# Half-token residual tiles, two pairs of chunks on the first token half ahead of the second half, and operand differences on VectorE

## The chip, the cores and the metric

The kernel runs on one core of a Trainium2 chip. The metric is the device time of one execution in microseconds (us). Three runs of the kernel before gave 1216.2, 1216.57 and 1218.2 us; the median is 1216.57 us. Views of the profile count time from the start of the profiled execution.

## What is computed

One inference step of a one-layer decoder: 1024 prompt tokens and 8 x 4 sample tokens, 1056 columns in all, 1024 features. A mixer (a state-space scan beside sliding-window attention) comes first, then an output projection with a residual add, then a feed-forward block:

```
def hybrid_layer(x, lp, ...):
    ...
    x = x + jnp.concatenate([y_ssd, y_att], axis=-1) @ lp['w_out']
    hn = rmsnorm(x, lp['norm2'])
    u, ffn_conv_new = causal_dwconv(hn @ lp['w_up'], ffn_conv_prev, lp['ffn_conv_w'], lp['ffn_conv_b'])
    gate, val = jnp.split(u, 2, axis=-1)
    x = x + (jax.nn.silu(gate) * val) @ lp['w_down']
```

The change touches the stretch from the output projection to the first chunks of `hn @ w_up`.

## The kernel before

**Layout.** Everything is feature-major: a tile holds 128 features on partitions and tokens along the free axis. The residual stream is eight tiles `acc[m]` of 128 x 1056. The tokens form two halves (`tp` 0 and 1, HT = 528 columns) of two quarters (QC = 264 columns). Each fp32 product is made of three matmuls on TensorE (PE): high by high, high by low, low by high. An operand is split by a copy on ScalarE (ACT), which makes the high part, and a subtraction on VectorE (DVE), which makes the low one.

**Output projection** (`out_piece`, matmuls at L147). A piece is one `m` and one quarter: 24 matmuls of 264 columns into one PSUM bank, then an add into `acc[m]` on VectorE (L771). Most pieces of the first token half stand in a table of steps (`PLAN`), among the last steps of the mixer; after the table follow the rest of the first half, `half_prep(0)`, and the sixteen pieces of the second half. `half_done` writes the finished half tile to DRAM (L833) and adds its square to a running sum (ACT at L839, VectorE at L840).

**Normalization and operands** (`half_prep(tp)`). `half_rstd` sums the squares over features with small matmuls (L845), takes the reciprocal root in short VectorE steps (L134 to L140, L847), and spreads it over partitions with six transposes on TensorE (L852) and two ACT copies (L854). Then eight VectorE instructions scale the half tiles in place (L864). The matrix product `hn @ w_up` is done as a two by two block scheme with seven block products, so seven operands are formed from the four blocks of (feature half) x (quarter): four blocks and differences of them. Each operand has four feature tiles: four ACT copies (L875), four VectorE subtractions (L876); four differences (`minus`, L880, on GpSimd, named POOL in the views) precede each of four operands. All work on 128 x 264 tiles.

**Up projection.** For each of 22 pairs `cp` of output chunks, `up_load` reads two 512 KB weight tiles into two buffers tagged "raw", and `up_operand(cp, j)` makes seven weight operands `au` (four differences and sums on GpSimd at L910 and L912, seven ACT copies at L922, seven VectorE subtractions at L923) in eight rotating slots. `product(cp, tp, j)` is 12 matmuls of 264 columns (L976), j = 0 to 6 for each half; j = 6 is put off until after j = 1 of the next half. Results are read out of PSUM by ACT (L990, L993, L996, L1004) and VectorE (L984, L986, L998) into two tiles `u` of the pair. When both halves are done, `conv` runs over each `u`: one ACT pass (L1016), two VectorE passes of 128 x 1072 (L1018), then SiLU or the final product (L1027).

**What sets the order.** The kernel is traced in program order; a scheduler then places each instruction in the queue of its engine, each queue runs strictly in order, and tiles come out of pools with a fixed number of buffers. The pool `yp` has eight buffers with tag "y"; the tiles `acc`, the tiles `u` and the conv results `c` share them. The program order around the change is: products of pair 0 on half 0, then `half_prep(1)`, then pair 0 on half 1, then pair 1 on both halves, and so on:

```
for cp in range(NPAIR):
    for tp in range(2):
        if (cp, tp) == (0, 1):
            half_prep(1)
```

Of the kernel before, what the change touches and what calls it, by code (L numbers as in the profile page):

```python
# [46 lines left out]
def kernel(ctx, tc, xT, wxbc, wkv, wq, wz, wout, wup, wdn, cols, rows, cst, idm,  # L47
# [711 lines left out]
    def out_load(m):  # L759
        if acc[m] is None:  # L760
            acc[m] = yp.tile([128, T], F32, tag="y", name="acc")
            sp.dma_start(out=acc[m], in_=xT[m])
        w[m] = load_unit(wout[m])

    def out_piece(m, q):
        if w.get(m) is None:
            out_load(m)
        a, b = q * QC, q * QC + QC
        ps = bank()[:, :QC]
        dense(ps, wl(w[m]), lambda h, k: yx[k][h][:, a:b], range(8))  # L770
        dve.tensor_tensor(out=acc[m][:, a:b], in0=acc[m][:, a:b], in1=ps, op=ALU.add)  # L771
# [58 lines left out]
    def half_done(m, tp, first):  # L830

        h = acc[m][:, tp * HT:tp * HT + HT]
# [26 lines left out]
    def half_prep(tp):  # L859

        rb = half_rstd(tp)
        for m in (4, 5, 6, 7, 0, 1, 2, 3):
            h = acc[m][:, tp * HT:tp * HT + HT]
            dve.scalar_tensor_tensor(out=h, in0=h, scalar=col(C_N2 + m), in1=rb, op0=ALU.mult, op1=ALU.mult)  # L864

        def quarter(r, c):
            return [acc[(0 if r else 4) + j][:, (2 * tp + c) * QC:(2 * tp + c) * QC + QC] for j in range(4)]
# [3 lines left out]
        def operand(name, src):  # L871
            hl = [x2p[tp].tile([128, 4, QC], F32R, tag=name + p, name=f"x2{p}") for p in "hl"]
            X2[tp][name] = hl
            for j in range(4):
                act.activation(out=hl[0][:, j], in_=src[j], func=AF.Copy)  # L875
                dve.tensor_tensor(out=hl[1][:, j], in0=src[j], in1=hl[0][:, j].bitcast(F32), op=ALU.subtract)  # L876

        def minus(o, p, q):
            for j in range(4):
                pool.tensor_tensor(out=o[j], in0=p[j], in1=q[j], op=ALU.subtract)  # L880
# [12 lines left out]

    nslot = [0]
# [3 lines left out]
    def up_load(cp):  # L898
        raws[cp] = [wr.tile([128, 1024], F32, tag="raw", name="raw") for _ in range(2)]
        for i in range(2):  # L900
            sp.dma_start(out=raws[cp][i], in_=wup[2 * cp + i])

    def up_operand(cp, j):

        ra, rb = raws[cp]
        a12, a11, a22, a21 = ra[:, 0:512], ra[:, 512:1024], rb[:, 0:512], rb[:, 512:1024]
        if j == 1:
            A[cp, "t"] = pt_.tile([128, 512], F32, tag="t1", name="t1")
        t = A.get((cp, "t"))
        minus = lambda o, p, q: pool.tensor_tensor(out=o, in0=p, in1=q, op=ALU.subtract)  # L910
        if j == 1:
            pool.tensor_tensor(out=t, in0=a21, in1=a22, op=ALU.add)  # L912
# [7 lines left out]
        w = wp.tile([128, 1024], F32R, tag=("uh", "ul")[nslot[0] % 2], name="au")  # L920
# [318 lines left out]
```

## Time and profile before

| | |
|---|---|
| median of three runs | 1216.57 us |
| profiled execution: its own time | 1216.3 us |
| its span, first to last instruction | 1214.5 us |
| mean granted TensorE clock | 0.976 |
| busy share PE / DVE / ACT / POOL | 96% / 71% / 42% / 32% |
| product matmuls of the up projection (L976) | 3696 |

The profiled execution took 1216.3 us, 1.8 us more than the span between its first and its last instruction, and 0.3 us less than the median. In rows of a view, `ps<-x2h,au 128x264 x12 | 1.2, 286 | 0.5 <-ACT u L990` reads: twelve instructions that write `ps` from `x2h` and `au`, 1.2 us busy in all, 286 ns each, 0.5 us of idle time on that engine just ahead of them, ended by the ACT instruction at line 990. A timeline row begins with its start and its length in us; idle time stands in brackets. Matmuls overlap, so their starts and not their lengths set the pace.

### The profile page before, as it was taken

The page shows a single profiled execution, that of the slowest core. Times are in us where ns is not written, and L with a number is a line of the kernel's source. Part 1 is how long each engine was busy: PE and PEld are TensorE (multiplying, and loading weights), DVE is VectorE, ACT ScalarE, POOL GpSimd, SP SyncE. Part 2 cuts the span into 40 slices and gives each one's busy share as a digit, 9 for nine tenths or more (in the row PEclk, how much of TensorE's full clock was granted, in tenths as well). Part 3 has the DMA queues.
Part 4 walks back from the last instruction along what each step waited for, and adds up shares of the span by engine and source line. Part 5 has one row for each costly group of instructions (what it writes and reads, how often), then busy time and mean ns, then how long its engine had stood idle before and what let it go on. Part 6 is the DMA issues. An engine that isn't in the chain of part 4 may idle for free.

```text
span 1214.5 us, 22163 instructions
## 1 busy us (share of the span) xinstructions
PE 1161.0 (96%) x8614; PEld 1113.6 (92%) x8614; DVE 865.3 (71%) x1732; ACT 508.7 (42%) x1013; POOL 385.7 (32%) x511
## 2 busy tenths in 40 slices
PE   8999999989989998499999999999999999999998
PEld 7998888869767998399999999999999999999998
DVE  7678857486797588866866666666666877777764
ACT  7344644454544343454545554554545322112110
POOL 0125444343443042733434343444443011101000
PEclk9999999999988999599999999999999999999999
DMA  8111112132645513022222222222222853423403
GB/s 289 62 62 57 36 49 66 26 105 70 184 138 157 177 54 136 1 71 71 76 84 73 87 72 88 71 88 72 88 72 88 289 182 125 139 89 110 146 9 144
DMA packets 50921, 121.48 MB, mean 100 GB/s; under 512 B 9072, under 2 KB 19824, under 8 KB 50800
## 3 DMA queue, kind: packets, MB, share of 16 engines
q1 hardware_dynamic: 50816, 120.07, 29.3%
q8 instruction: 67, 1.10, 0.4%
q14 instruction: 38, 0.31, 0.1%
HBM read 93.81 MB, written 27.26 MB: 100 GB/s over the span
## 4 chain that ended last, share of the span: by engine, by line
PE 85%; DVE 6%; POOL 3%; DMA 2%; issue 2%; ACT 1%; SPq 0%; POOLq 0%; ACTq 0%
PE ps L976 36%; PE ps L147 34%; PE ps L199 6%; POOL acc L880 2%; PE ps L525 1%; PE sc L503 1%; DVE acc L864 1%; PE yy L653 1%; DVE x2l L876 1%; PE ps L517 1%; PE st L660 1%; PE two L147 1%; PE yy L655 0%; DVE au L923 0%; DMA xr<-in_xT 0%
## 5 line engine op out<-in xcount | busy, mean ns | idle before, releaser
L976 PE MATMUL ps<-x2h,au 128*128 128x264 f32 x2464 | 457.1, 286 | 10.9 <-ACT u L990 6.1
L976 PEld LDWEIGHTS ps<-x2h,au 128*128 128x128 f32 x2464 | 385.8, 190 | 12.2 <-ACT u L990 6.4
L976 PE MATMUL ps<-x2l,au 128*128 128x264 f32 x1232 | 351.1, 286 | 5.3 <-DVE x2l L876 5.3
L976 PEld LDWEIGHTS ps<-x2l,au 128*128 128x128 f32 x1232 | 233.6, 190 | 6.5 <-DVE x2l L876 6.5
L1088 DVE TENSOR_TENSOR acc<-acc,ps 128x352 f32<-128x352 f32 x264 | 131.4, 517 | 66.3 <-PE ps L147 65.7
L147 PE MATMUL ps<-xh,uh 128*128 128x264 f32 (+3 forms) x528 | 164.4, 318 | 8.1 <-ACT xh L182 5.5
L147 PE MATMUL ps<-gl,uh 128*128 128x352 f32 x528 | 170.1, 322 | 0.0
L147 PE MATMUL ps<-gh,ul 128*128 128x352 f32 x528 | 169.9, 322 | 0.0
L147 PE MATMUL ps<-gh,uh 128*128 128x352 f32 x528 | 167.8, 322 | 0.1
L147 PE MATMUL ps<-xl,uh 128*128 128x264 f32 (+3 forms) x528 | 166.3, 315 | 0.6 <-POOL xl L180 0.4
L147 PE MATMUL ps<-xh,ul 128*128 128x264 f32 (+3 forms) x528 | 165.1, 313 | 0.0
L116 ACT ACTIVATE uh<-raw 128x1024 fp32r<-128x1024 f32 (+3 forms) x59 | 55.8, 953 | 189.7 <-PE ps L147 171.2
L1018 DVE SCALAR_TENSOR_TENSOR c<-u,colt,c 128x1072 f32<-128x1072 f32 x88 | 120.0, 1364 | 1.1 <-ACT c L1016 0.8
L147 PEld LDWEIGHTS ps<-xh,uh 128*128 128x128 f32 x528 | 101.8, 195 | 12.4 <-ACT xh L182 5.8
L923 DVE TENSOR_TENSOR au<-raw,au 128x512 fp32r<-128x512 f32 x110 | 76.0, 704 | 43.5 <-ACT au L922 43.4
L147 PEld LDWEIGHTS ps<-xl,uh 128*128 128x128 f32 x528 | 102.8, 195 | 2.6 <-POOL xl L180 0.9
L147 PEld LDWEIGHTS ps<-xh,ul 128*128 128x128 f32 x528 | 102.8, 195 | 1.6 <-issue 0.7
L147 PEld LDWEIGHTS ps<-gl,uh 128*128 128x128 f32 x528 | 99.2, 188 | 0.5 <-DVE gl L180 0.2
L147 PEld LDWEIGHTS ps<-gh,ul 128*128 128x128 f32 x528 | 99.3, 188 | 0.0
L147 PEld LDWEIGHTS ps<-gh,uh 128*128 128x128 f32 x528 | 98.8, 188 | 0.3 <-ACT gh L179 0.3
L922 ACT ACTIVATE au<-raw 128x512 fp32r<-128x512 f32 x110 | 68.4, 625 | 23.1 <-PE ps L976 11.3
L923 DVE TENSOR_TENSOR au<-t,au 128x512 fp32r<-128x512 f32 x44 | 43.5, 988 | 35.4 <-PE ps L976 19.0
(291 smaller groups left out, 1973.3 us busy)
## 6 DMA issues: line engine op xcount, KB each, us to landing
raw<-in_wup SPq DMA_DIRECT2D x44, 512.0 KB, 3.5
gr<-gd SPq DMA_DIRECT2D x22, 528.0 KB, 5.1
gd<-c SPq DMA_DIRECT2D x22, 512.0 KB, 2.6
raw<-in_wdn SPq DMA_DIRECT2D x22, 512.0 KB, 4.2
raw<-in_wout SPq DMA_DIRECT2D x12, 512.0 KB, 3.8
acc<-in_xT SPq DMA_DIRECT2D x8, 528.0 KB, 5.9
accd<-acc SPq DMA_DIRECT2D x16, 264.0 KB, 2.0
acc<-accd SPq DMA_DIRECT2D x8, 528.0 KB, 8.0
```

Source lines behind the costliest of these rows:

```text
L116: act.activation(out=hi, in_=raw, func=AF.Copy)
L147: pe.matmul(out=ps, lhsT=w(a, k), rhs=x(b, k), start=first and k == ks[0] and i == 0, stop=last and k == ks[-1] and i == 2)
L199: pe.matmul(out=ps[:m, :n], lhsT=x[k][c][:, a:a + m], rhs=w[k // nk][b][:, o:o + n], start=k == 0 and i == 0, stop=k == 7 and i == 2)
L503: pe.matmul(out=sb[:, v, c].rearrange("p i k -> p (i k)"), lhsT=qT[a][r, c], rhs=kT[b][r, o:o + 256], start=i == 0, stop=i == 2)
L517: pe.transpose(out=pt[:, h], in_=P[:, h], identity=ident)
L525: pe.matmul(out=po[64 * v:64 * v + 64, 0:256].rearrange("p (c q) -> p c q", c=2), lhsT=(vall[:, t - i] if i or not t else vdif[:, t - 1])[ ...
L880: pool.tensor_tensor(out=o[j], in0=p[j], in1=q[j], op=ALU.subtract)
L922: act.activation(out=w[:, 0:512], in_=src, func=AF.Copy)
L923: dve.tensor_tensor(out=w[:, 512:1024], in0=src, in1=w[:, 0:512].bitcast(F32), op=ALU.subtract)
L976: pe.matmul(out=ps, lhsT=wgt[:, 512 * a + 128 * k:512 * a + 128 * k + 128], rhs=xx[b][:, k], start=opens and k == 0 and i == 0, stop=k == ...
L1018: dve.scalar_tensor_tensor(out=c[:, 0:n], in0=u[:, j:j + n], scalar=col(C_FW + 3 * m + j), in1=c[:, 0:n], op0=ALU.mult, op1=ALU.add)
L1088: dve.tensor_tensor(out=o, in0=o, in1=ps[:, :PC], op=ALU.add)
```

## The change

It does three things.

1. **Half-token tiles.** `acc[m]` of 128 x 1056 is replaced by `hacc[m // 2, tp]`, a tile of 128 x 2 x 528 for two feature tiles and one token half. There are again eight of them, of the same size; the four of the first half carry nothing of the second half. Each half tile is loaded by its own DMA (16 of 264 KB in place of 8 of 528 KB). Copies, subtractions and differences of `half_prep` run over two feature tiles at once: 14 + 14 + 8 instructions of 528 elements in place of 28 + 28 + 16 of 264, for each half.
2. **Order of the pairs.** A list `SETS` of weight sets takes the place of the loop over pairs: set 0 is pair 0 on half 0; set 1 is pair 1 on both halves; set 2 is pair 0 again, on half 1, with its weights loaded and split a second time; from set 3 on each pair is done on both halves as before. `half_prep(1)` stays in program order behind pair 0 on half 0; pair 1 on half 0 now follows it.
3. **Engine.** The differences of `half_prep`, and the differences and sums of the weights of sets 0, 1 and 2, go from GpSimd to VectorE.

The core of the diff:

```diff
+    def half(m, tp):
+        if (m // 2, tp) not in hacc:
+            hacc[m // 2, tp] = yp.tile([128, 2, HT], F32, tag="y", name="acc")
+        return hacc[m // 2, tp][:, m % 2]
...
+        if acc[m] != tp:
+            acc[m] = tp
+            sp.dma_start(out=half(m, tp), in_=xT[m][:, tp * HT:tp * HT + HT])
...
-            for j in range(4):
-                act.activation(out=hl[0][:, j], in_=src[j], func=AF.Copy)
-                dve.tensor_tensor(out=hl[1][:, j], in0=src[j], in1=hl[0][:, j].bitcast(F32), op=ALU.subtract)
+            for j in range(2):
+                h, l = (t[:, 2 * j:2 * j + 2] for t in hl)
+                act.activation(out=h, in_=src[j], func=AF.Copy)
+                dve.tensor_tensor(out=l, in0=src[j], in1=h.bitcast(F32), op=ALU.subtract)
         def minus(o, p, q):
-            for j in range(4):
-                pool.tensor_tensor(out=o[j], in0=p[j], in1=q[j], op=ALU.subtract)
+            for j in range(2):
+                dve.tensor_tensor(out=o[j], in0=p[j], in1=q[j], op=ALU.subtract)
...
+    SETS = [(0, [(0, 0)]), (1, [(1, 0), (1, 1)]), (0, [(0, 1)])]
+    SETS += [(cp, [(cp, 0), (cp, 1)]) for cp in range(2, NPAIR)]
...
+        e = dve if n < 3 else pool
+        minus = lambda o, p, q: e.tensor_tensor(out=o, in0=p, in1=q, op=ALU.subtract)
...
+    for n, (cp, groups) in enumerate(SETS):
+        for g in groups:
+            more = g == groups[-1] and n + 1 < len(SETS)
+            if more:
+                up_load(n + 1)
+            done = n >= 2 if cp == 0 else g[1] == 1
+            for j in range(6):
+                product(n, *g, j)
+                if j == 1 and last:
+                    product(*last[0], 6)
+                    if last[1]:
+                        conv(last[0][1], 1)
+                if more:
+                    up_operand(n + 1, j)
+            if more:
+                up_operand(n + 1, 6)
+            if done:
+                conv(cp, 0)
+            last = (n, *g), done
+            if g == (0, 0):
+                half_prep(1)
```

**Where the queues change.** In the rows below a name before the arrow is written and names behind it are read; `au_...` is one weight operand, `x2h_...` and `x2l_...` the high and low part of a token operand, `ps_...` a PSUM bank. On TensorE before, at the end of `half_rstd(1)`: the transposes (L852) are followed at once by the first product on the second half (`x2h_5790`).

```order
L976 MATMUL ps_5681<-x2l_5114,au_5642 128x264
L976 MATMUL ps_5681<-x2h_5113,au_5642 128x264
L852 MATMUL ps_5772<-idt_85,v2_5757 128x88 x3
L852 MATMUL ps_5777<-idt_85,v2_5757 128x88 x3
L976 MATMUL ps_5880<-x2h_5790,au_5626 128x264
```

Only four of pair 0's seven products on half 0 stand ahead of these transposes in the kernel before. In the changed kernel the transposes (L858) stand in the middle of pair 1's product with `au_5729` on half 0:

```order
L988 MATMUL ps_5862<-x2h_5089,au_5729 128x264
L858 MATMUL ps_5774<-idt_85,v2_5759 128x88 x3
L858 MATMUL ps_5779<-idt_85,v2_5759 128x88 x3
L988 MATMUL ps_5862<-x2h_5089,au_5729 128x264
L988 MATMUL ps_5862<-x2l_5090,au_5729 128x264
L988 MATMUL ps_5862<-x2h_5089,au_5729 128x264
```

All seven products of pair 0 and four and three quarters of pair 1's (141 matmuls) now stand between the output projection and the transposes. Fifteen matmuls further down the first reads of the second half follow (`x2h_5792` is its operand B11, `x2h_5814` its operand B21), with pair 1's last product on half 0 (`au_5749`) behind them:

```order
L988 MATMUL ps_5848<-x2l_5098,au_5746 128x264
L988 MATMUL ps_5848<-x2h_5097,au_5746 128x264
L988 MATMUL ps_5948<-x2h_5792,au_5657 128x264
L988 MATMUL ps_6016<-x2h_5814,au_5712 128x264
L988 MATMUL ps_6083<-x2h_5792,au_5962 128x264
L988 MATMUL ps_5848<-x2h_5105,au_5749 128x264
```

So three single matmuls that need the second half were put ahead of twelve that need only the first. On VectorE before, in `half_prep(1)`: scaling (L864), then subtractions for the low parts, with the differences elsewhere (on GpSimd).

```order
L140 SCALAR_TENSOR_TENSOR v_5757<-rs 88x6
L864 SCALAR_TENSOR_TENSOR acc<-acc,colt,ssum_5204 128x528 x8
L876 TENSOR_TENSOR x2l<-acc,x2h 128x264 x15
L923 TENSOR_TENSOR au<-t_5925,au 128x512
L876 TENSOR_TENSOR x2l<-acc,x2h 128x264 x8
```

And now, with the scaling at L870, the low parts at L883 and the differences at L887:

```order
L140 SCALAR_TENSOR_TENSOR v_5759<-rs 88x6
L935 TENSOR_TENSOR au<-raw,au 128x512
L1010 TENSOR_TENSOR u<-u,ps 128x264
L924 TENSOR_TENSOR t_5993<-raw 128x512
L996 TENSOR_TENSOR u<-s_5902,ps 128x264
L870 SCALAR_TENSOR_TENSOR acc<-acc,colt,ssum_5166 128x528 x8
L996 TENSOR_TENSOR u<-s_5875,ps 128x264
L883 TENSOR_TENSOR x2l<-acc,x2h 128x528 x5
L887 TENSOR_TENSOR acc<-acc 128x2x264
```

Work for weight set 2 (L935, L924) and evictions (L1010, L996) moved in ahead of the scaling, and the differences stand between the low parts.

More of the change, by code (lines that the diff above doesn't have):

```diff
@@ L757, in ssd_split @@
             split(fm[4 * g + j][:, a:b], yx[4 + 2 * g + j], None, a, b)
[L759 to L763, printed above, removed]
+    hacc = {}
+    def half(m, tp):
+        if (m // 2, tp) not in hacc:
+            hacc[m // 2, tp] = yp.tile([128, 2, HT], F32, tag="y", name="acc")
+        return hacc[m // 2, tp][:, m % 2]
     def out_piece(m, q):
+        tp = q // 2
         if w.get(m) is None:
-            out_load(m)
-        a, b = q * QC, q * QC + QC
+            w[m] = load_unit(wout[m])
+        if acc[m] != tp:
+            acc[m] = tp
+            sp.dma_start(out=half(m, tp), in_=xT[m][:, tp * HT:tp * HT + HT])
         ps = bank()[:, :QC]
-        dense(ps, wl(w[m]), lambda h, k: yx[k][h][:, a:b], range(8))
-        dve.tensor_tensor(out=acc[m][:, a:b], in0=acc[m][:, a:b], in1=ps, op=ALU.add)
+        dense(ps, wl(w[m]), lambda h, k: yx[k][h][:, q * QC:q * QC + QC], range(8))
+        o = half(m, tp)[:, (q % 2) * QC:(q % 2) * QC + QC]
+        dve.tensor_tensor(out=o, in0=o, in1=ps, op=ALU.add)
     pcc.__exit__(None, None, None)
@@ L830, in half_done @@
     def half_done(m, tp, first):
-        h = acc[m][:, tp * HT:tp * HT + HT]
+        h = half(m, tp)
         sp.dma_start(out=accd[m][:, tp * HT:tp * HT + HT], in_=h)
@@ L862, in half_prep @@
         for m in (4, 5, 6, 7, 0, 1, 2, 3):
-            h = acc[m][:, tp * HT:tp * HT + HT]
+            h = half(m, tp)
             dve.scalar_tensor_tensor(out=h, in0=h, scalar=col(C_N2 + m), in1=rb, op0=ALU.mult, op1=ALU.mult)
         def quarter(r, c):
-            return [acc[(0 if r else 4) + j][:, (2 * tp + c) * QC:(2 * tp + c) * QC + QC] for j in range(4)]
+            return [hacc[(0 if r else 2) + j, tp][:, :, c * QC:c * QC + QC] for j in range(2)]
         b11, b12, b21, b22 = quarter(0, 0), quarter(0, 1), quarter(1, 0), quarter(1, 1)
@@ L896, with up_load, up_operand @@
     raws = {}
[L898 to L899 removed]
+    def up_load(n):
+        raws[n] = [wr.tile([128, 1024], F32, tag="raw", name="raw") for _ in range(2)]
         for i in range(2):
[L901 to L905 removed]
+            sp.dma_start(out=raws[n][i], in_=wup[2 * SETS[n][0] + i])
+    def up_operand(n, j):
+        ra, rb = raws[n]
         a12, a11, a22, a21 = ra[:, 0:512], ra[:, 512:1024], rb[:, 0:512], rb[:, 512:1024]
         if j == 1:
[L908 to L910 removed]
+            A[n, "t"] = pt_.tile([128, 512], F32, tag="t1", name="t1")
+        t = A.get((n, "t"))
+        e = dve if n < 3 else pool
+        minus = lambda o, p, q: e.tensor_tensor(out=o, in0=p, in1=q, op=ALU.subtract)
         if j == 1:
[L912 removed]
+            e.tensor_tensor(out=t, in0=a21, in1=a22, op=ALU.add)
         elif j == 2:
@@ L960, in u_tiles, with product @@
             U[cp].append(u)
-    def product(cp, tp, j):
-        if j == 0 and tp == 0:
+    def product(n, cp, tp, j):
+        if j == 0 and cp not in U:
             u_tiles(cp)
```

32 lines of the change are left out of this document (7 added, 25 removed).

## The prediction

> **What bounds the kernel now.** I read the page first. Its slices show TensorE (PE) at 90% or more nearly everywhere in the later two thirds, but for one dip, in which the granted clock falls too:
>
> ```profile
> PE   8999999989989998499999999999999999999998
> PEclk9999999999988999599999999999999999999999
> ```
>
> A slice is 30.4 us, so the 4 and the 5 stand at 486 to 516 us. Next I cut that stretch into windows, for the product matmuls alone (L976):
>
> ```profile
> 474.60:479.20 4.60, 4.52 (x36) 4.33 (x36) 1.00 0.57 185
> 479.20:515.13 35.93, 14.36 (x58) 12.05 (x59) 0.62 0.09 33
> 580.00:915.00 335.00, 335.00 (x2748) 335.00 (x2747) 1.00 0.23 80
> ```
>
> The last row gives the undisturbed price: 335.0 / 2748 = 0.1219 us per matmul, with PE busy throughout; nothing before the down projection can be gained there. The first two rows hold 36 + 58 = 94 matmuls in 40.5 us. At the undisturbed price they take 11.5 us. The timeline of PE shows two small things that stay whatever the change does, and what else ended its waits:
>
> ```profile
> 474.62 0.28 PE L976 MATMUL ps<-x2h,au 128*128 128x264 f32 x1
> 481.71 1.10 PE L845 MATMUL ps<-ones,ssum 128*88 128x1 f32 x12 [2.57 <-DVE ssum L840]
> 486.26 0.67 PE L852 MATMUL ps<-idt,v 88*128 88x88 f32 x6 [1.89 <-DVE v L140]
> 488.72 0.59 PE L976 MATMUL ps<-x2h,au 128*128 128x264 f32 x1 [1.79 <-ACT x2h L875]
> 493.36 0.59 PE L976 MATMUL ps<-x2l,au 128*128 128x264 f32 x1 [4.06 <-DVE x2l L876]
> 510.36 0.59 PE L976 MATMUL ps<-x2h,au 128*128 128x264 f32 x1 [6.09 <-ACT u L990]
> ```
>
> Sums and transposes take 1.10 + 0.67 = 1.8 us. So the gap loses 40.5 - 11.5 - 1.8 = **27.2 us**. Two chains make it. One is the statistics and the second half's operands. The other is a buffer: the read-out of the very first product waits for a difference of `half_prep(1)` to release a "y" tile,
>
> ```profile
> 509.92 0.39 ACT L990 ACTIVATE u<-ps 128x264 f32<-128x264 f32 x1 [0.47 <-POOL acc L880]
> ```
>
> although that product's matmuls began at 474.6, when the output projection was done. In between VectorE (DVE) and GpSimd (POOL) do the operands, and the clock is halved:
>
> ```profile
> 488.70:515.10 26.40, 12.64 (x45) 10.52 (x46) 24.70 (x38) 12.78 (x32) 21.41 (x22) 0.50 0.00 1
> L876 DVE TENSOR_TENSOR x2l<-acc,x2h 128x264 fp32r<-128x264 f32 x28 | 18.2, 709 | 1.7 <-ACT x2h L875 1.7
> L880 POOL TENSOR_TENSOR acc<-acc 128x264 f32<-128x264 f32 x16 | 18.1, 1163 | 8.8 <-DVE x2l L876 8.8
> L864 DVE SCALAR_TENSOR_TENSOR acc<-acc,colt,ssum 128x528 f32<-128x528 f32 x8 | 5.5, 764 | 1.2 <-ACT ssum L854 1.2
> ```
>
> (First row: PE 12.64 us, DVE 24.70, POOL 21.41 busy of 26.40, clock 0.50.)
>
> **The change part by part.** *Half-token tiles* take the buffer chain away. The first half's four tiles are free when `half_prep(0)` has read them, and its last subtractions end at 460.6 here:
>
> ```profile
> 459.15 1.45 DVE L876 TENSOR_TENSOR x2l<-acc,x2h 128x264 fp32r<-128x264 f32 x4
> 460.87 0.70 DVE L840 TENSOR_TENSOR ssum<-ssum,sq 128x528 f32<-128x528 f32 x1
> 461.49 1.21 DVE L119 TENSOR_TENSOR ul<-raw,uh 128x1024 fp32r<-128x1024 f32 x1
> ```
>
> Four tiles serve `u` of pairs 0 and 1, so both can be read out during `half_prep(1)`. These rows also price VectorE without GpSimd beside it: 0.36 us per 264 elements, and 0.62 us per 528 (from 460.87 to 461.49). `half_prep` then costs 14 + 8 instructions of 0.62, 13.6 us, on VectorE alone, against 18.2 us of VectorE with 18.1 us of POOL interleaved.
>
> *First half's preparation and the output projection* (430.0 to 474.6): PE never idles there, and VectorE is busy 40.55 of 44.6 us.
>
> ```profile
> 430.00:474.60 44.60, 44.60 (x370) 44.60 (x369) 40.55 (x63) 21.83 (x46) 21.75 (x20) 1.00 0.24 85
> ```
>
> VectorE takes over sixteen differences as eight and set 0's four sums, 12 x 0.62 = 7.4 us, and loses the slow-down of its own subtractions, about 28 x 0.35 = 9.8 us if they slow there as above. I price this at nothing. The cover is PSUM: eight banks (pools of 3 and 5), a piece of 24 x 0.1219 = 2.9 us each. Bounds: -1.5 to +2 us, the latter if VectorE ran behind by 2 us at the end.
>
> *DMA.* Eight more residual loads of half the size, and pair 0's two weight tiles again. Loads of the second half now stand ahead of two output-weight loads on SyncE's queue; those were issued at 404.32 and are first read at 437.49, so I price them at nothing, bounds -0.5 to +1. Slight shifts of pieces within the mixer's last steps: nothing, -1.5 to +1.5.
>
> ```profile
> 404.32 2.26 SPq L115 DMA_DIRECT2D raw<-in_wout  x2
> 437.49 1.06 ACT L116 ACTIVATE uh<-raw 128x1024 fp32r<-128x1024 f32 x1 [0.33 <-PE ps L147]
> ```
>
> *Cover in the new order.* From 474.6 PE has 84 matmuls of pair 0 and 57 of pair 1 ahead of the transposes, and the sums: 474.6 + 141 x 0.1219 + 1.8 = 493.6. Does anything delay it? VectorE's queue between the last eviction of the projection and the scaling holds 14 instructions of 512 elements (0.61 by the rate above) for weight sets 0 to 2, a sum of squares (0.62), five evictions of about 0.4 and thirteen small steps that follow each other by 0.2 (rows below): 8.5 + 0.6 + 2.0 + 2.6 = 13.7 us. The last eviction came at 477.4, VectorE lagging; with less lag it is 475.0, so the queue ends at 488.7 to 491.1 unless it waits.
>
> ```profile
> 476.72 0.76 DVE L771 TENSOR_TENSOR acc<-acc,ps 128x264 f32<-128x264 f32 x2
> 484.67 0.16 DVE L139 TENSOR_TENSOR rs<-rs 88x6 f32<-88x6 f32 x1
> 484.87 0.16 DVE L140 SCALAR_TENSOR_TENSOR rs<-rs 88x6 f32<-88x6 f32 x1
> 511.26 0.42 DVE L998 TENSOR_TENSOR u<-u,ps 128x264 f32<-128x264 f32 x1
> ```
>
> The add at L924 for set 1 is now on VectorE and waits for a weight load; evictions and the statistics are queued behind it.
>
> ```profile
> 476.24 0.33 SPq L901 DMA_DIRECT2D raw<-in_wup  x1
> 478.10 0.33 SPq L901 DMA_DIRECT2D raw<-in_wup  x1
> raw<-in_wup SPq DMA_DIRECT2D x2, 512.0 KB, 4.2
> ```
>
> Even issued as late as here that load lands at 478.1 + 4.2 = 482.3, and the 11 us of the queue behind it end at 493.3, still by the transposes. Term zero, up to +3.
>
> *What is late next.* After the transposes PE has 15 matmuls, to 495.4. Two ACT copies (0.67) end at 494.3; the eight scalings run to 494.3 + 5.5 = 499.8. The first matmul of the second half wants two scalings and an ACT copy of 0.65: 496.3. The second wants B21, whose tiles are scaled fifth and sixth: 494.3 + 6 x 0.69 + 0.65 = 499.1. PE waits from 495.4 to 499.1, less one matmul: **3.6 us** (2 to 6), while twelve matmuls that need neither stand behind.
>
> ```profile
> 486.74 0.67 ACT L854 ACTIVATE ssum<-ps 128x264 f32<-128x264 f32 x2 [5.61 <-PE ps L852]
> 464.44 0.65 ACT L839 ACTIVATE sq<-acc 128x528 f32<-128x528 f32 x1 [1.67 <-DVE acc L771]
> ```
>
> *Operands against products.* From 499.8 VectorE needs 13.6 us for the second half's operands, about 4.3 for seven instructions of set 2 and 1.5 for evictions, 19.4 us; PE has 12 + 168 matmuls, 21.9 us. They are nearly level, so PE waits where an operand comes late. T1 is the clear one: its low part is VectorE's tenth instruction after the scaling, about 506.5, and PE, through B11 and B21, is there at 505. Then each difference, copy and subtraction passes DVE, ACT, DVE. **3.5 us** (0 to 8).
>
> *Convolutions.* Pair 1 and pair 0 now end together, so four convs meet in one stretch where there were two per pair. Eight passes of 1.35 and two products of 1.2 are 13.2 us, with set 3's and 4's subtractions queued among them, inside about 20 us of PE work; PE's queue wants set 3's first low part while three conv passes stand ahead of it. **4 us** (0 to 8).
>
> ```profile
> L1018 DVE SCALAR_TENSOR_TENSOR c<-u,colt,c 128x1072 f32<-128x1072 f32 x71 | 95.8, 1349 | 0.5 <-ACT c L1016 0.3
> L923 DVE TENSOR_TENSOR au<-raw,au 128x512 fp32r<-128x512 f32 x89 | 60.8, 697 | 37.6 <-ACT au L922 37.5
> ```
>
> *Clock.* Two gaps show when it falls. The first has 1.2 us of PE work in 3.2 us, and the next 3.4 us run at half clock:
>
> ```profile
> 422.50:425.70 3.20, 1.21 (x16) 1.00 (x14) 1.14 (x2) 0.64 (x1) 0.00 (x0) 1.00 0.23 84
> 426.30:429.70 3.40, 3.40 (x18) 3.40 (x17) 1.58 (x10) 0.00 (x0) 0.00 (x0) 0.50 0.00 0
> 482.70:488.70 6.00, 2.33 (x20) 1.95 (x19) 4.27 (x15) 1.09 (x3) 1.28 (x1) 0.92 0.00 0
> ```
>
> The second, 2.5 us idle up to 481.7, did not halve it at once (0.92 after). An episode of 3.4 us costs half, 1.7 us. My 3.6 us wait is like the first: **2 us** for one episode and a bit (0 to 6). [...]
>
> **The sum.** New losses: 3.6 + 3.5 + 4 + 2 = 13.1 us. Gain: 27.2 - 13.1 = 14.1 us. From the profiled execution's own 1216.3 us (span 1214.5) that is 1202.2; the median is 0.3 above it, so **1202.5 us**.
>
> **The rivals.** *Covered almost wholly* (gain 18 to 25 us): waits of VectorE and PE overlap and convs hide. Losses of 3.6 and 1 leave 1216.6 - 22.6 = 1194 us. For it: 19.4 against 21.9 us above. Against it: the three single matmuls placed early.
>
> *The half clock stays* (gain 0 to 8 us): PE is fed by VectorE in small portions and never gets a full window of work. Before, 26.4 us at 0.50 is such a stretch. If pair 1's and pair 0's second halves (168 matmuls) all run at half price, they cost 168 x 0.1219 = 20.5 us more, while PE then runs behind VectorE and the waits on operands and convs disappear: 27.2 - 3.6 - 20.5 = 3.1 us gain, 1213.5 us. Against it: between 499 and 521 PE would be busy over 80% of the time, where that stretch has 48%.
>
> *Slower: each early set waits for its weights.* Sets 0, 1 and 2 have one half of products (84 x 0.1219 = 10.2 us) to make the next set's seven operands, where a pair has had 20.5. A weight load (4.2) and two rounds of difference, copy and subtraction (about 2 x 1.9) are 8 us before the fourth operand. If buffers released only when a half ends, three sets would each stall about 10 us: 30 + 3.6 - 27.2 = 6.4 us slower, 1223 us. It decides when raw tiles come free more than 2 us after the sixth operand. Against it: eight slots for seven operands, and the raw rows above, issued while products still ran. That the change does not do what it says is excluded by the queues: pair 1's products do stand ahead of the second half's.
>
> **How the numbers follow.** A measurement of this kernel can tell about 0.2%, 2.4 us, from no change. Forecast (gain 9 to 18): 0.60. Covered: 0.20. Half clock: 0.13, of which 0.05 lie within 2.4 us of no change. Slower: 0.07. So faster 0.60 + 0.20 + 0.08 = 0.88, same 0.05, slower 0.07. The covered case reaches to 1193 but for 0.05 of it; 1213 takes in the forecast's larger losses (27.2 - 23.6 of gain left) and half of the half-clock case. Outside are 0.05, 0.07 and 0.07. Range **1193 to 1213**.
>
> **What would show it.** Right: the read-out of the first product within 1 us of its last matmul; PE without a gap over 2 us until about 495; one wait of 3 to 4 us that ends at an ACT copy of B21; then waits under 2 us on x2l until about 521, and waits on `au` behind conv passes until about 545; half clock for under 5 us. Wrong: PE waiting on `au` of set 1 before 495, a half clock over 10 us, or a PE gap ahead of 474.

## The result, and the profile after

The changed kernel takes 1209.93 us (median of 5 executions, 1206.2 to 1212.86) against 1218.2 us before in the same comparison. The ratio is 0.9933, with a 95% interval from 0.9906 to 0.9959: faster by 0.67%, about 8.3 us. The forecast was 1202.5 us with a range from 1193 to 1213, and a gain of 14.1 us. The profiled execution of the changed kernel takes 1211.65 us (span 1209.9).

The page's slices (30.2 us each) show the deep dip gone. In its place PE has three slices at 8, from 484 to 575 us, and the clock an 8 in the first of them:

```profile
PE   7999999989989999888999999999999999999998
PEclk9999999999988899899999999999999999999999
```

The windows of the product matmuls alone (line 988 in this kernel; columns: stretch, its length, PE busy and matmuls, weight loads, granted clock, DMA share, GB/s):

```profile
477.77:496.30 18.53, 17.56 (x142) 17.19 (x142) 1.00 0.36 122
496.30:507.40 11.10, 7.40 (x37) 6.68 (x38) 0.69 0.01 1
507.40:520.00 12.60, 12.30 (x98) 11.88 (x98) 1.00 0.00 1
520.00:580.00 60.00, 53.37 (x422) 51.68 (x421) 1.00 0.26 85
580.00:915.00 335.00, 335.00 (x2748) 335.00 (x2747) 1.00 0.24 79
```

The first row is the cover: 142 matmuls in 18.5 us, in which only the sums and transposes are missing from a busy PE. The second is the wait that was forecast, with the clock at 0.69. The fourth is the news: in 60 us PE is idle for 6.6 us, in a stretch where the kernel before had no idle time once its dip was over:

```profile
515.13:523.00 7.87, 7.87 (x67) 7.87 (x66) 1.00 0.00 0
523.00:540.00 17.00, 17.00 (x142) 17.00 (x141) 1.00 0.29 95
540.00:580.00 40.00, 40.00 (x330) 40.00 (x330) 1.00 0.20 67
```

The last row of the changed kernel, from 580 us on, has the same busy time and matmuls as before.

To compare runs without what lies ahead of the change, the rest of this text uses one measure: the start of the first product matmul is zero, and the table says when 168, 336 and 672 product matmuls have been issued, that is, when the next one starts (one, two and four pairs of work; at 0.1219 us each they would take 20.5, 41.0 and 81.9 us). "The 168th" below stands for this point, and so on. The next column is the time from the 6900th to the 7100th matmul of the program, the entry of the down projection. All are from the traces, one execution each. The changed kernel, e4 and e5 have the same work up to the 168th and show it at 27.6 us each; the changed kernel and e5 still agree at the 672nd.

| kernel | 168th | 336th | 672nd | down entry | ratio to before, 95% |
|---|---|---|---|---|---|
| before | 49.6 | 70.1 | 111.1 | 28.9 | 1 |
| changed | 27.6 | 51.4 | 99.7 | 32.5 | 0.9933 (0.9906 to 0.9959) |
| e1: old order of pairs | 33.1 | 53.6 | 94.7 | 28.4 | 0.9871 (0.9848 to 0.9895) |
| e2: differences on GpSimd | 33.5 | 64.2 | 109.2 | 32.3 | 1.0014 (0.9998 to 1.0031) |
| e3: preparation written first | 28.4 | 54.3 | 98.9 | 32.1 | 0.9906 (0.9882 to 0.9930) |
| e4: no passes for pair 0 | 27.6 | 51.2 | 95.1 | 32.7 | 0.9902 (0.9883 to 0.9921) |
| e5: slot counter from 1 | 27.6 | 51.4 | 99.7 | 29.1 | 0.9901 (0.9881 to 0.9922) |
| e6: e1 with preparation first | 32.6 | 53.0 | 94.1 | 28.4 | 0.9872 (0.9853 to 0.9891) |
| e7: half tiles alone | 40.9 | 62.3 | 103.3 | 28.4 | 0.9922 (0.9901 to 0.9944) |
| e8: VectorE differences alone | 45.7 | 66.2 | 107.2 | 28.7 | 0.9939 (0.9918 to 0.9960) |
| e10: pair 0's second half later | 27.1 | 49.4 | 95.6 | 28.4 | 0.9892 (0.9870 to 0.9913) |
| e11: e1, weight sums on GpSimd | 34.7 | 55.7 | 96.7 | 29.4 | 0.9887 (0.9864 to 0.9911) |
| e12: e1 with filler matmuls | 31.2 | 53.3 | 94.4 | 28.5 | 0.9875 (0.9858 to 0.9891) |

In the changed kernel the dip gives back 111.1 - 99.7 = 11.4 us, and the entry of the down projection takes 32.5 - 28.9 = 3.6 us of that: 7.8 us, which agrees with the 8.3 us of the medians. The two profiled executions differ by less, 1216.3 - 1211.65 = 4.7 us; where the rest went is told under the term on half tiles below. The table also holds the surprise of this study: e1, which leaves the pairs in their old order, is faster than the changed kernel, and the two intervals don't touch.

### The profile page after: what moved, and what is told of

It is laid out like the page before. It is cut to its first block, busy times and chain, and to the rows that moved or that the text cites. A ratio compares the mean times of both kernels' runs of the same rounds, so it can differ in the third digit from the quotient of the medians.

```text
span 1209.9 us, 22111 instructions
## 1 busy us (share of the span) xinstructions
PE 1162.5 (96%) x8614; PEld 1114.6 (92%) x8614; DVE 864.8 (71%) x1739; ACT 506.2 (42%) x992; POOL 346.8 (29%) x471
## 4 chain that ended last, share of the span: by engine, by line
PE 82%; DVE 7%; DMA 5%; ACT 2%; POOL 1%; issue 1%; SPq 0%; POOLq 0%; ACTq 0%; DVEq 0%
PE ps L147 36%; PE ps L988 32%; PE ps L199 6%; PE ps L525 1%; DMA raw<-in_wup 1%; PE sc L503 1%; DMA xr<-in_xT 1%; DVE au L935 1%; PE yy L653 1%; DVE x2l L883 1%; PE ps L517 1%; PE st L660 1%; DMA Cs<-ead 1%; DMA acc<-accd 1%; DVE ul L119 1%
## 5 line engine op out<-in xcount | busy, mean ns | idle before, releaser
L1102 DVE TENSOR_TENSOR acc<-acc,ps 128x352 f32<-128x352 f32 x264 | 131.5, 517 | 69.9 <-PE ps L147 66.6
L116 ACT ACTIVATE uh<-raw 128x1024 fp32r<-128x1024 f32 (+3 forms) x59 | 55.7, 952 | 192.5 <-PE ps L147 178.6
L935 DVE TENSOR_TENSOR au<-raw,au 128x512 fp32r<-128x512 f32 x115 | 78.7, 699 | 39.9 <-ACT au L934 39.7
L934 ACT ACTIVATE au<-raw 128x512 fp32r<-128x512 f32 x115 | 71.2, 625 | 35.0 <-PE ps L147 9.1
L935 DVE TENSOR_TENSOR au<-t,au 128x512 fp32r<-128x512 f32 x46 | 41.6, 904 | 36.2 <-PE ps L988 19.0
```

The lines of the kernel that those rows point to most:

```text
L116: act.activation(out=hi, in_=raw, func=AF.Copy)
L934: act.activation(out=u[:, 0:512], in_=src, func=AF.Copy)
L935: dve.tensor_tensor(out=u[:, 512:1024], in0=src, in1=u[:, 0:512].bitcast(F32), op=ALU.subtract)
L1102: dve.tensor_tensor(out=o, in0=o, in1=ps[:, :PC], op=ALU.add)
```

## The experiments

Only the lines that carry each edit are shown.

### e1: half tiles and VectorE differences, old order of the pairs

```diff
-    SETS = [(0, [(0, 0)]), (1, [(1, 0), (1, 1)]), (0, [(0, 1)])]
-    SETS += [(cp, [(cp, 0), (cp, 1)]) for cp in range(2, NPAIR)]
+    SETS = [(cp, [(cp, 0), (cp, 1)]) for cp in range(NPAIR)]
```

> Half-token tiles and differences on VectorE as in the changed kernel, but the pairs in the old order (0, 1, 2, ..., each on both halves). The changed kernel's median is 1209.9 us, the one before 1218.2. Measure inside a run, free of what lies ahead: the time from the last matmul of the output projection to the 4000th matmul of the program; 111 us before, 100 in the changed kernel. Theory A (two chains made the gap: the buffer chain is removed by the half tiles, the statistics and operands of the second half are only covered by the order): the read-out of the first product comes within 1 us of its matmuls, PE works through pair 0's first half and then idles and creeps behind VectorE from about 10 us after the projection until about 38 us after it; about 18 us of the 27 stay lost, but no set runs on half the products and the convolutions do not meet, so nothing is given back later: 103 us, time about 1210 (1207 to 1214). Theory B (the order of the pairs carries the gain, the tiles only make it possible): 110 us, 1217. Theory C (the buffer chain was the whole gap): 92 us, 1200.

Measured: 94.7 us to the 672nd product and 1203.8 us (median of 6). That lies between A (which by this measure stood for 103) and C, nearer to C's number, and far from B. C's reason, that the buffer chain was the whole gap, does not hold: e7 below takes that chain away and still needs 103.3 us. In the timeline of PE the chain of the second half is open to view, as A said; two waits make most of it:

```profile
491.72 0.39 PE L987 MATMUL ps<-x2h,au 128*128 128x264 f32 x1 [2.75 <-ACT x2h L882]
495.74 0.59 PE L987 MATMUL ps<-x2l,au 128*128 128x264 f32 x1 [3.63 <-DVE x2l L883]
```

But A took PE to creep behind VectorE until the operands were all done. It doesn't: from the 100th product (23.4 us) to the 168th (33.1) it needs 9.7 us where 8.3 would be full rate. The whole loss is 33.1 - 20.5 - 1.8 (sums and transposes) = 10.8 us, all inside pair 0. Behind it the windows of the product matmuls show full rate, which the changed kernel reaches only at about 578 us:

```profile
523.00:580.00 57.00, 57.00 (x469) 57.00 (x468) 1.00 0.25 85
```

The new order pays less for the chain (27.6 us to the 168th), but 99.7 - 27.6 = 72.1 us for the next 504 products, where e1 needs 61.6. So this order of the pairs, one of the change's three parts, costs 5.0 us on balance.

### e7 and e8: each of the other two parts alone

e7 is e1 with all differences on GpSimd again; e8 is the kernel before with the differences on VectorE.

```diff
-                dve.tensor_tensor(out=o[j], in0=p[j], in1=q[j], op=ALU.subtract)
+                pool.tensor_tensor(out=o[j], in0=p[j], in1=q[j], op=ALU.subtract)
...
-        e = dve if n < 3 else pool
+        e = pool
```

> The half-token tiles alone: old order of the pairs, all differences on GpSimd. From the first product to the 672nd: 111.1 us before, 94.7 with tiles and VectorE differences. Theory A (the two parts each carry some of it: the buffer chain held the first product's read-out for about 35 us, and GpSimd's differences stretch the operands by about 8 us): 102 us (100 to 105), time about 1211. Theory B (with VectorE free of weight sums the old order can stand GpSimd's differences; they only hurt in the new order, where sets 1 and 2 must be ready in half the time): 95 to 97 us, 1205.

> The kernel before with the differences of half_prep and of weight sets 0 to 2 on VectorE: full-token tiles, old order. From the first product to the 672nd: 111.1 us before. Theory A (the read-out of the first product still waits for a difference of half_prep(1) to release its tile, but that difference comes earlier: 16 differences of 0.36 in place of 1.16 us each, subtractions at 0.36 in place of 0.71): the release comes 8 us earlier, 102 to 104 us, time about 1211. Theory B (the buffer chain is what counts, and VectorE becomes the longer chain): 109 to 111 us, 1217 to 1219.

Measured: e7 103.3 us and 1211.0, as A said. e8 107.2 us and 1212.5, between its A and B; the mechanism is A's. In e8 the read-out of the first product still waits for a tile, as the timeline of ScalarE shows; its matmuls began at 477.9:

```profile
508.58 0.68 ACT L991 ACTIVATE u<-ps 128x264 f32<-128x264 f32 x2 [0.52 <-DVE x2l L876]
```

That is 30.7 us after the first matmul, and 35.3 before (509.92 - 474.6): the faster differences bring the release 4.6 us forward, not 8. Alone the tiles give 7.8 us and the engine 3.9; together (e1) 16.4, more than the sum of the two. With the engine alone the wait for the tile stands, as the row shows; with the tiles alone PE still waits for the second half's operands, 2.75 + 3.63 + 2.14 + 2.11 us in its four longest waits.

### e2: differences on GpSimd in the new order

Its edit is that of e7, made in the changed kernel.

> The changed kernel with all operand differences back on GpSimd (those of half_prep and of weight sets 0 to 2). Theory A (GpSimd beside VectorE slows VectorE's subtractions from 0.62 to about 1.2 us per 528 elements, and its own differences take about 2 us each): the second half's operands take about 26 us in place of 17, PE waits on them 6 to 9 us more; from the projection's end to the 4000th matmul 107 us (100 in the changed kernel), time 1216 (1213 to 1221). Theory B (VectorE is the bound between 500 and 523 us, busy 20 of 20, and a GpSimd that stands idle can only relieve it): 97 us, 1206. Also open: the first half's differences at 430 to 475 us, which I priced at nothing; if PE waits there, the stretch from its first product matmul on grows by 1 to 4 us.

Measured: 109.2 us and 1219.7, no gain left at all. A named the mechanism; by the trace it was short by 2 us, and the time lies in its range. B is out. The groups of VectorE and GpSimd between 476 and 530 us show the price (busy us, mean ns of one):

```profile
L883 DVE TENSOR_TENSOR x2l<-acc,x2h 128x528 fp32r<-128x528 f32 x14 | 18.6, 1380 | 0.0
L887 POOL TENSOR_TENSOR acc<-acc 128x528 f32<-128x528 f32 x8 | 13.5, 1703 | 7.9 <-DVE x2l L883 7.9
```

The same rows in the changed kernel, where both run on VectorE:

```profile
L883 DVE TENSOR_TENSOR x2l<-acc,x2h 128x528 fp32r<-128x528 f32 x14 | 9.5, 701 | 0.0
L887 DVE TENSOR_TENSOR acc<-acc 128x528 f32<-128x528 f32 x8 | 5.5, 700 | 0.0
```

Fourteen subtractions take 18.6 us beside GpSimd and 9.5 without, 9.1 us more; the eight differences took VectorE 5.5 us. Eight weight sums went to GpSimd in the same stretch, another 5.5 us, and other VectorE instructions became longer as well. Taken over all groups that both kernels have, by count and mean, VectorE's instructions are longer by 15.7 us, against 11.1 us of work that it was rid of: moving work to an idle engine slowed the busy one by more than it took off. The trace shows both engines' records side by side:

```profile
509.26 1.79 POOL L887 TENSOR_TENSOR acc<-acc 128x528 f32<-128x528 f32 x1
509.79 1.83 DVE L883 TENSOR_TENSOR x2l<-acc,x2h 128x528 fp32r<-128x528 f32 x1
511.01 1.79 POOL L887 TENSOR_TENSOR acc<-acc 128x528 f32<-128x528 f32 x1
```

The difference ends at 511.05, the subtraction 0.57 us later at 511.62, the next difference 1.18 us after that. So the records overlap and their ends alternate, in steps close to what one takes by itself: in the changed kernel such a subtraction takes 0.70 us, and a GpSimd sum 1.29 (the one at 550.43, with VectorE idle from 550.52 on). That reads as if the two took turns here and each record contained a wait for the other; what makes them wait no run shows.

### e11: only the weight sums on GpSimd

```diff
-        e = dve if n < 3 else pool
+        e = dve if n < 1 else pool
```

> Half tiles, old order of the pairs, half_prep's differences on VectorE, the sums of weight sets 1 and 2 back on GpSimd. From the first product to the 672nd: 94.7 us with all of them on VectorE, 103.3 with all on GpSimd. Theory A (any GpSimd sum beside VectorE's operands slows VectorE's subtractions from 0.62 to over 1 us and comes late itself): 96 to 99 us, time about 1206. Theory B (VectorE is saturated from 489 to 512 us, so four sums fewer free 2.4 us there and four sums of GpSimd disturb little): 92 to 93.5 us, time about 1202.

Measured, in e1's order: 96.7 us and 1204.2, A. Three of set 1's four sums on GpSimd fall among the operands' subtractions and take their mean from 704 ns in e1 to 781:

```profile
L883 DVE TENSOR_TENSOR x2l<-acc,x2h 128x528 fp32r<-128x528 f32 x14 | 10.5, 781 | 0.0
```

The 2.0 us by which it is behind e1 can be read from the traces; the medians (1204.2 and 1203.8) can't tell them apart.

### e3 and e6: the second half's preparation written first

e3 is the changed kernel, e6 is e1, each with the same move:

```diff
+    half_prep(1)
     last = None
     for n, (cp, groups) in enumerate(SETS):
...
-            if g == (0, 0):
-                half_prep(1)
```

> The changed kernel with the second half's preparation written ahead of the first set's products, not behind them: its sums and transposes stand about 84 product matmuls behind the projection, not 141, and the scaling ahead of set 2's first steps. Theory A (the 3.5 us wait on scaling and ACT copies, the half clock after it and the 4 us of operands against products all come from the preparation starting too late): scaling starts about 7 us earlier, the wait and the half clock go, the operands run ahead of PE; from the projection's end to the 4000th matmul 91 to 94 us (100 in the changed kernel), time about 1202. Theory B (VectorE is saturated, so what the preparation gains the weight sets 1 and 2 lose): PE waits on au instead, 98 to 101 us, 1208 to 1211. Whatever the result, the stretch up to the projection holds the same instructions in the same order as the changed kernel: if the 4.7 us lost there against the kernel before come from the order, every such run shows them; if from where the half clock happens to fall, they vary by several us from run to run.

> Half tiles and VectorE differences in the old order of the pairs, with the second half's preparation written ahead of pair 0's products, so that the sums stand 43 matmuls behind the projection in place of 60. In the old order the whole loss (94.7 us from the first product to the 672nd, of which 81.9 are matmuls and 1.8 sums) lies within pair 0, and its length is set by the chain sums, root, scaling, operands on VectorE. Theory A: the chain starts 2 us earlier and ends 2 us earlier, 92 to 93 us, time 1202. Theory B (as with the preparation first in the new order, the evictions and set 1's first sum, which waits for its weight load, hold VectorE's queue, so the chain starts no earlier): 94 to 96 us, 1204 to 1205.

Measured: e3 98.9 us and 1208.5; e6 94.1 us and 1204.4. Both numbers are B's. In e3 the scaling does come earlier, but by 2.7 us and not 7 (493.73 against 497.31, which is 16.8 and 19.5 us after the first product), since set 1's subtractions stand between the steps of the root; the 3.5 us wait goes, and PE waits elsewhere:

```profile
489.38 0.39 PE L988 MATMUL ps<-x2h,au 128*128 128x264 f32 x1 [2.58 <-DVE u L996]
516.89 0.39 PE L988 MATMUL ps<-x2l,au 128*128 128x264 f32 x1 [1.36 <-DVE x2l L883]
```

It is 0.8 us behind the changed kernel at the 168th product and 2.9 us at the 336th, and 0.8 us ahead at the 672nd. That is B's account: what one chain gains another loses.

In e6 the number is B's but the chain did what A said. The scaling starts 10.8 us after the first product and not 13.2 as in e1, and the last of the second half's low parts 32.6 us after it and not 34.9, so the whole chain is 2.3 us earlier. After 100 products PE is still 2.2 us ahead of e1, after 168 only 0.5. In between it is the half clock that differs. It lasts two cells in both runs, from 17.5 to 24.3 us after the first product in e6 and from 16.4 to 23.2 in e1, so in e6 it covers a cell in which PE already has work throughout: 17 matmuls, where e1 issues 30 at the same place of its chain (e6 first, then e1; columns as in the windows under e12):

```profile
500.60:504.00 3.40, 3.40 (x17) 3.40 (x17) 3.40 (x6) 1.80 (x4) 0.00 (x0) 0.50 0.00 0
499.60:503.00 3.40, 3.40 (x30) 3.40 (x30) 3.40 (x6) 1.79 (x4) 0.00 (x0) 1.00 0.00 0
```

The 13 matmuls between them are worth 1.6 us at 0.1219 each, about what e6 lost. Whether it would keep the 2.3 us without this cell was not tried.

### e4 and e10: four convolutions that meet

e4 leaves work out, e10 moves pair 0's second half behind pair 2, with the slot counter of e5.

```diff
-        for j in range(1, 3):
+        for j in range(1, 3 if cp else 1):
```

```diff
-    SETS = [(0, [(0, 0)]), (1, [(1, 0), (1, 1)]), (0, [(0, 1)])]
-    SETS += [(cp, [(cp, 0), (cp, 1)]) for cp in range(2, NPAIR)]
-    nslot = [0]
+    SETS = [(0, [(0, 0)]), (1, [(1, 0), (1, 1)]), (2, [(2, 0), (2, 1)]), (0, [(0, 1)])]
+    SETS += [(cp, [(cp, 0), (cp, 1)]) for cp in range(3, NPAIR)]
+    nslot = [1]
```

> The changed kernel without the two VectorE passes (L1030) of each of pair 0's two convolutions: the values of pair 0 are therefore those of the first tap alone. 4 x 1.33 = 5.3 us of VectorE work leave the stretch from 523 to 547 us. Theory A (four convolutions meeting on VectorE delay the low parts of sets 3 and 4 and through them the raw buffers and the next weight loads, 5.7 us of PE between the 3700th and the 4000th matmul): 4 us of it go, from the projection's end to the 4000th matmul 96 us (100 in the changed kernel), time 1206. Theory B (PE waits there on weight loads issued late for other reasons, and on GpSimd's first sum of set 3, 1.7 us): under 1 us goes, 99 to 100 us, 1209 to 1210.

> The changed kernel with pair 0's second half placed behind pair 2 in place of behind pair 1, and the slot counter started at 1 (which gave back 3.5 us at the down projection). Pair 1's and pair 0's convolutions then no longer meet; pair 2's and pair 0's do, but 20 us later, when the second half's operands are long done on VectorE. From the first product to the 672nd: 99.7 us with the slot counter alone. Theory A (what is lost between the 336th and the 672nd product, 7 us, comes from the second half's operands, set 2's and 3's differences and four convolutions falling into the same 25 us on VectorE): 94 to 97 us, time 1203 to 1206. Theory B (the loss belongs to a set that has one half of products to cover the next set's weight load and operands, and to two pairs of convolutions within 30 us, wherever they stand): it moves and stays, 99 to 101 us, time 1208.

Measured: e4 95.1 us to the 672nd and 1206.7; without 5.3 us of VectorE work PE is 4.5 us earlier, where A said 4. e10 95.6 us and 1204.5, again A. By the 1000th product e10 has lost another 0.95 us, so 3.1 us of its 4.1 are for good; it is then still 1.9 us behind e1 (136.6 against 134.7 us). What remains in both, 3.0 us in e4 between the 336th and the 672nd product, isn't from these passes.

### e5: the parity of the weight slots

```diff
-    nslot = [0]
+    nslot = [1]
```

> The changed kernel with the counter of weight slots started at 1 in place of 0. The new order has 23 weight sets of seven operands, 161, an odd number, so the two slot tags end on the other one than with 22 sets; SyncE's queue at the entry of the down projection then issues its weight loads, the convolution's reload and the eight loads of the residual in another sequence, and PE there loses 3.6 us. Starting at 1 gives SyncE the sequence of the kernel before back. Measure: from the 6900th to the 7100th matmul 32.5 us in the changed kernel and in the other runs with 23 sets, 28.9 before and 28.4 with 22 sets. Theory A (the parity is the cause): 28.4 to 29.0, time 1206.3. Theory B (the loads are late because everything ahead runs closer together, or the half clock falls there by chance): 32 to 33, 1209.9.

Measured: 29.1 us at the entry of the down projection where the changed kernel takes 32.5, and 1208.5 (the intervals of the two ratios overlap; the stretch itself tells). All four runs with 23 sets and a counter from 0 show 32.1 to 32.7; those with 22 sets, and e10 with 23 and a counter from 1, 28.4 to 29.4. The list of SyncE's instructions ahead of the residual's loads differs so, the changed kernel first and e5 second:

```
L115 DMA raw<-in_wdn 128x1024 x2
L1041 DMA gd<-c 128x1024
L1042 DMA gd<-gs 128x32
L115 DMA raw<-in_wdn 128x1024
L1083 DMA gr<-gd 128x1056 x2
L115 DMA raw<-in_wdn 128x1024 x2
L1069 DMA out_fco<-fcot 128x792
L1083 DMA gr<-gd 128x1056
L1109 DMA dec<-decs 128x72
L1089 DMA acc<-accd 128x1056 x8

L115 DMA raw<-in_wdn 128x1024 x3
L1041 DMA gd<-c 128x1024
L1042 DMA gd<-gs 128x32
L115 DMA raw<-in_wdn 128x1024
L1083 DMA gr<-gd 128x1056 x2
L115 DMA raw<-in_wdn 128x1024
L1069 DMA out_fco<-fcot 128x792
L1109 DMA dec<-decs 128x72
L1089 DMA acc<-accd 128x1056 x8
```

In the first, one weight load has moved behind the stores of the convolution, and a third reload of `gd` stands ahead of the eight loads of the residual. PE then waits for a bank whose eviction (line 1102) adds that residual; these are the waits of PE from 935 to 985 us in the changed kernel:

```profile
PE ps L147 <- DVE acc L1102: 2.3, 1, 2.3
PE ps L147 <- ACT gh L179: 0.6, 1, 0.6
```

and in e5, where the wait on L1102 is gone:

```profile
PE ps L988 <- DVE u L998: 0.7, 1, 0.7
PE ps L147 <- ACT gh L179: 0.2, 1, 0.2
```

All four runs with 23 sets and a counter from 0 show this wait, 2.0 to 3.1 us of it; e1, e5, e10 and the kernel before do not. Three of the four, the changed kernel among them, also have 3.4 us of half clock there.

### e12: filler matmuls in the gap

The base is e1.

```diff
+        if tp:
+            fl.append(bank())
+            for i in range(24):
+                pe.transpose(out=fl[0][:, :88], in_=b3(v[:88, 1, i % 6:i % 6 + 1], 88, 128), identity=ident[:88, :88])
...
+                if tp and name == "B11":
+                    for i in range(12):
+                        pe.matmul(out=fl[0][:, :QC], lhsT=h[:, 0, 0:128], rhs=h[:, 1], start=True, stop=True)
```

> Half tiles, VectorE differences, old order of the pairs, and 48 added matmuls whose result nobody reads (24 small transposes behind the second half's transposes, 24 products of an operand with itself behind the first two copies), placed where PE waits for the second half's operands. Without them PE is busy 0.39 and 0.46 of 3.4 us in the two grid windows ahead of the half clock at 492.8 to 499.6, in which 3.04 us of products then run at half price. From the first product to the 672nd 94.7 us without them. Theory A (the clock of a window follows PE's busy share in the window before, and falls only below about half): no half clock between 485 and 505, 1.5 to 1.9 us less, 92.8 to 93.2, time 1202. Theory B (the clock has no part in the length of the gap, because VectorE sets it): 94.5 to 94.9, 1204. Theory C (the filler delays the products behind it): over 95.

Measured: the half clock of the gap is gone, as A said, but the 672nd product starts at 94.4 us, next to B's 94.5 to 94.9, and the time is 1202.7 (ratio 0.9875; e1 has 0.9871). The windows of e1 by the clock's own grid (columns: stretch, length, PE, PEld, DVE, ACT and POOL busy, clock, DMA share, GB/s):

```profile
489.40:492.80 3.40, 0.39 (x1) 0.19 (x1) 3.26 (x5) 1.17 (x3) 0.00 (x0) 1.00 0.00 0
492.80:496.20 3.40, 0.46 (x2) 0.46 (x3) 3.40 (x6) 2.50 (x5) 0.00 (x0) 0.50 0.00 0
496.20:499.60 3.40, 3.04 (x14) 2.73 (x14) 3.40 (x7) 1.48 (x4) 0.00 (x0) 0.50 0.00 0
```

and the same place in e12:

```profile
490.40:493.80 3.40, 2.48 (x23) 2.30 (x22) 3.40 (x7) 1.29 (x2) 0.00 (x0) 1.00 0.00 0
493.80:497.20 3.40, 2.69 (x22) 2.48 (x21) 3.40 (x7) 2.36 (x4) 0.00 (x0) 1.00 0.00 0
497.20:500.60 3.40, 2.38 (x17) 1.95 (x16) 3.40 (x6) 1.82 (x4) 0.00 (x0) 1.00 0.00 0
```

At the 168th product e12 is 1.9 us ahead, at the 336th 0.3: PE at full speed only reaches VectorE's next operand sooner, and VectorE is busy 3.40 of 3.40 us in each of these windows. Here the half clock cost at most 0.3 us, since VectorE set the pace; in e6, where it fell on a cell in which PE had work throughout, it cost about 1.6.

## Why the prediction was right, and where it was not

The direction and the mechanism held, and the time lies in the range; the gain was 8.3 us where 14.1 were forecast. That is just under the 9 to 18 us that the prediction gave to its own case, and next to the 0 to 8 us of its half-clock rival, whose mechanism did not come. Two terms were wrong, the convolutions by 3.3 us and the queue order of a later stage by 3.6; that the time is in the range all the same is owed to the range's width. Point by point:

**The gap loses 27.2 us: right.** In the changed kernel 94 products have been issued 12.4 us after the first began, before 40.6. That is 28.2 us less, of which 0.7 are transposes that now come later: 27.5. The first read-out was to come within 1 us of its last matmul; the twelfth matmul starts at 477.77 + 11 x 0.1219 = 479.1:

```profile
479.44 0.38 ACT L1002 ACTIVATE u<-ps 128x264 f32<-128x264 f32 x1
497.31 5.51 DVE L870 SCALAR_TENSOR_TENSOR acc<-acc,colt,ssum 128x528 f32<-128x528 f32 x8
499.49 0.39 PE L988 MATMUL ps<-x2h,au 128*128 128x264 f32 x1 [1.15 <-ACT x2h L882]
502.20 0.81 PE L988 MATMUL ps<-x2h,au 128*128 128x264 f32 x2 [2.33 <-ACT x2h L882]
```

**A wait of 3.6 us at the copy of B21, and 2 us of half clock: right.** The last two rows are 3.5 us of waits, at the places named, in two pieces where one was expected (the forecast's 495.4 to 499.1 are 498.3 to 502.2, because the projection ended 3.1 us later). With the clock, 27.6 - 20.5 - 1.8 = 5.3 us are lost up to the 168th product; 5.6 were forecast. The half clock lasted 6.8 us, longer than the 5 us named as a sign, but cost only 5.3 - 3.5 = 1.8.

**Operands against products, 3.5 us: right.** 51.4 - 27.6 - 20.5 = 3.3 us between the 168th and the 336th.

**Convolutions, 4 us: mis-sized.** Between the 336th and the 672nd product 99.7 - 51.4 - 41.0 = 7.3 us are lost. The step costed the passes on VectorE against PE's queue, and e4 shows that this part is 4.5 us. It left out what a late operand does next. The timeline of the changed kernel, from the loads of set 3 to those of set 4:

```profile
523.12 0.93 SPq L912 DMA_DIRECT2D raw<-in_wup  x2
529.63 1.72 POOL L924 TENSOR_TENSOR t<-raw 128x512 f32<-128x512 f32 x1 [1.01 <-DMA raw<-in_wup]
532.07 0.39 PE L988 MATMUL ps<-x2h,au 128*128 128x264 f32 x1 [1.29 <-ACT au L934]
536.70 3.65 DVE L1030 SCALAR_TENSOR_TENSOR c<-u,colt,c 128x1072 f32<-128x1072 f32 x2
543.82 2.13 SPq L912 DMA_DIRECT2D raw<-in_wup  x2
547.23 0.63 ACT L934 ACTIVATE au<-raw 128x512 fp32r<-128x512 f32 x1 [3.62 <-DMA raw<-in_wup]
```

Two raw tiles serve the weights, so a set's load is issued when the last subtraction of the set before has read them. Set 2's are done at about 523, set 3's stand among the passes from 523.61 to 545, and set 4's load goes out at 543.82. Each set starts late because the one before ended late, until a few pairs have worn it off at about 578 us. That this chain makes the 3.0 us that stay in e4 was read from the trace and not tried.

**DMA and SyncE's order, nothing: wrong.** The prediction looked at the queue in the projection. The 3.6 us (3.5 by e5 against the changed kernel) arose 450 us later, at the down projection: 23 sets of seven operands end on the other slot, and so another queue order; e5 shows it. The total forecast has no term for it.

**Half-tiles in the projection and the shifts of pieces ahead of it, nothing: right, though the profile seemed to deny it.** In the changed kernel's profile the first product starts 3.1 us later than before. But from the 2250th matmul to the first product the runs with half tiles take from 146.6 us (e11) to 153.2 (e5); the changed kernel's execution took 151.0. Over thirteen runs that time follows the half clock in the stretch, 13.7 to 30.7 us of it, by 0.33 us for each (correlation 0.95). e8, which has the old tiles, took 149.8 where the profile of before shows 147.4 with 17.1 us of half clock. So the execution that the sum started from, 1216.3 us, was a lucky one: the medians of before in the later comparisons are 1218.2 to 1220.1, and its granted clock, 0.976, is near the top of the 0.969 to 0.977 of those runs.

**The rivals.** "Covered almost wholly" was rightly put second: the cover held until 498, but VectorE had no room for what follows. "Half clock stays" did not come: 6.8 us of it, then full rate. "Each early set waits for its weights" was placed too early: sets 0 to 2 were in time, and its mechanism, loads that wait for raw tiles, struck sets 3 and 4.

So the sum was 27.2 - 13.1; by the traces it is 27.2 - (5.3 + 3.3 + 7.3) - 3.6 = 7.7 us. And what the prediction never asked is whether the cover is worth its price. It took the gap as two chains to be covered by the order. In e1 the half tiles and the engine shorten both chains, the uncovered rest is 10.8 us, and nothing is given back later: 1203.8 us. e6 and e12, built on it, are as fast; the intervals of e10 and e11 overlap with its own.

## What to carry to other kernels

Before work is moved to cover a wait, shorten the wait first and price the cover alone: here two of three parts gave 16.4 us in the changed stretch, and the third, the cover, took 5.0 of them and about 3.5 more elsewhere, which a slot counter started at 1 gives back. When an engine is saturated, look for what it delays that in turn frees a buffer and issues the next load; by the trace here the delay travelled from set to set. And when a loop gains an odd number of steps over alternating buffers, compare the queue order in the stages behind it, however far.

## What the runs showed of the hardware

**The clock beside PE's busy share.** All half-clock records of a run lie on a grid of 3.413 us and are one to eight cells long, but for the last, which the program's end cuts. I cut the thirteen traces into these cells and compared PE's busy share in one with the clock of the next. From each trace's first clock record on (9 to 12 us from the start), a cell at full clock with less than 45% busy was followed by half clock in 63 of 63 cases, one with 45 to 60% in 31 of 62, one with more in 13 of some 4,200. At half clock, cells with less than 85% busy stayed at half in 37 of 37; of the 137 with over 95%, 104 returned to full. The traces of the kernel before and the changed one alone give 9 of 9, 6 of 11 and 2 of 647 at full clock, and 10 of 10 and 17 of 21 at half. These are counts of this program's runs and not a rule for another. Four cells of the changed kernel (columns: stretch, length, PE busy, clock, DMA share, GB/s):

```profile
493.80:497.20 3.40, 3.40 (x33) 1.00 0.38 152
497.20:500.60 3.40, 1.52 (x11) 1.00 0.00 0
500.60:504.00 3.40, 1.58 (x5) 0.50 0.00 0
504.00:507.40 3.40, 3.40 (x18) 0.50 0.02 5
```

The longest idle time here is 2.33 us, and PE was busy 1.52 us of the cell ahead of the half clock. The first cells of half clock in the kernel before, e3 and e5 begin 28.3, 27.9 and 27.2 us after their first matmul, and in the changed kernel 98.6 us, although all four do the same in that stretch: they don't stand at one place of the program. If the grid falls otherwise in each run, this would also explain the spread of the runs, since a half-full stretch can then fall on one cell or on two; that reading rests on the correlation above and was not tried.

**GpSimd beside VectorE**: 1380 against 701 ns on average for the same subtraction with eight differences and two sums of GpSimd among fourteen, and 781 against 704 with three sums (e11 and e1).
